# Folding a norm's factor into weights and evictions, and moving shared products into the expert pairs

## The chip, the cores and the metric

The kernel runs on one core of one Trainium2 chip. The metric is the device time of one launch in microseconds; less is better. The kernel before was timed three times: median 508.37 us, 507.75 to 508.88 us. One execution was recorded by the hardware profiler; every row shown below comes from it.

## The reference

One layer of a hybrid decoder on 512 tokens of width 1024, all in 32-bit floats. Cut to what matters here:

```python
h = h + rms_norm(mix, post_mix_norm)              # after attention and short convolution
t = rms_norm(h, pre_ffn_norm)                     # g_ffn: one factor per feature
g_idx  = top1(softmax(t @ w_group_router + b))    # one of 4 groups
e_idx  = top2 of the group's 8 experts            # weights normalised, times the group's
routed = sum over the 2 experts of  (silu(t @ w_gate[e]) * (t @ w_up[e]) * weight) @ w_down[e]
shared = (silu(t @ w_sh_gate) * (t @ w_sh_up)) @ w_sh_down
h = h + rms_norm(routed + shared, post_ffn_norm)
```

There are 32 experts of hidden width 256 and one shared expert of the same width. An expert's gate, up and down weights are 1 MB each.

## The kernel before

Tokens lie in four chunks of 128 (index c). The kernel computes projections and convolution (to about 95 us), attention (to about 185 us), the output projections (`pco`, `pao`), and then the part that the change touches:

- *Second norm.* For each chunk `chain_gen` adds the residual (`mix`), takes the sum of squares on ACT, raises it to -1/2 on GpSimd (`sst`), and multiplies the chunk by this factor per token and by `g_ffn` per feature in one DVE instruction (`x<-mix,sst,gb`). The result is stored in DRAM (`t_d`) for the gathers.
- *Router.* `router_gen` transposes the chunk on the tensor engine (`ptT`), copies it to `tT`, and multiplies by the router's weights (`plT`, then `plg`).
- *Routing.* `route` works on the DVE, first for chunks 0 and 1, then for 2 and 3: best group, two best experts, and, with small products (`pps`, `ptb`), the place of each token in its expert's list. It ends with the overflow tables (`code`), for experts with more than 64 tokens. Its scratch is the tile `rs`.
- *Shared expert.* `shared_gen` computes its gate and up products (`psh`: for each chunk 32 products, from the weight tiles (32, 0) and (32, 1) and from `tT`). They fill the tensor engine while routing goes on. Its down products (`psd`) come later in blocks, into the tiles `sho`.
- *Expert pairs.* `pairs_gen` treats two experts at a time, j and j + 16, each with up to 64 tokens, side by side in the tensor engine. Per pair: the gathered tokens `xg` are transposed (`pxt`) into `wk`; sixteen gate-up products follow in two halves, i = 0 and 1 (`pgu`); silu and weighting; the next pair's transposes; the hidden layer's transposes (`pht`, evicted by ACT into `wk`); eight down products (`pdn`, out to `yb`); and an indirect DMA sends the rows to `y_d`. The last pair stays on the chip (`ys`).
- *Tail.* `last_gen` adds up, chunk by chunk in PSUM (`pca`), the shared part (`inject`: a product with the identity), the last pair's rows (a product with a selection `sel`), and the two routed rows of each token, read back from `y_d` and added on the DVE (`kk`). Then the third norm: squares on ACT, the product with `g_post` (`tm`) and the variance (`var`) on the DVE, the power on GpSimd (`rf`), and a multiply-add with the residual `hb` on the DVE, stored to `out`.

*What sets the order.* All stages are generators. `run` asks each, in the order of its priority, when it could go on by a model of the engines (`Progress`), and lets the first go that can; so the order on each engine is fixed when the program is built. Buffers are 25 slots of 1 MB. `rel` gives slots back, and `pump` hands them in turn to the queue of weight loads: on SP, in a fixed order, each load behind the last use of the slot that it takes. A tile's name (e, i) is expert e's gate-up half 0 or 1, or its down weights (2); 32 is the shared expert.

Nearly all instructions bear one of two lines in the profile, L159 (the wrapper of the engines) and L314 (`pe`, the tensor engine), so they are told apart by the names of their tiles.

Of the kernel before, what the change touches and what calls it, by code (L numbers as in the profile page):

```python
# [45 lines left out]
S_AT = 2  # L46
S_GO = 2
# [118 lines left out]
def hymba_kernel(ctx: ExitStack, tc: tile.TileContext, xT, xmT, x, meta, cpk, pos, wqkv, wconv, wuq, wukv,  # L166
# [214 lines left out]
    Y.dma_start(mt[:NMETA, :D], meta)  # L381
    Y.dma_start(posi, pos)
# [528 lines left out]
    def finish(c):  # L911
# [25 lines left out]
        if c == NT - 1:  # L937
            rel(A["b"])
            Y.dma_start(wrt, wr)

# [4 lines left out]
    def out_split_gen():  # L945
# [10 lines left out]
        Y.dma_start(late["gb"][:, D:2 * D], g_ffn[None, :].to_broadcast([P, D]))  # L956
# [6 lines left out]
        keep(0)  # L963

# [38 lines left out]
    def attn_out_gen(c, mg):  # L1003
# [19 lines left out]
        if c == NT - 1:  # L1023
            rt["rs"], rt["xg"], sh["hs"] = take(["rs", "xg", "hs"], *(wo[k] for k in range(4)), *A["mg"])
# [4 lines left out]
    def chain_gen(c, ss):  # L1029
        gb, m = late["gb"], mix(c)  # L1030
# [12 lines left out]
        V.scalar_tensor_tensor(tt(c), m, sst[:, c, 2:3], gb[:, D:2 * D], op0=OP.mult, op1=OP.mult)  # L1043
        spawn(router_gen(c), 0 if c == NT - 1 else P_ROUTER)

    def router_gen(c):
# [14 lines left out]
        yield every(at(*(tT(k, c * P, (c + 1) * P) for k in (0, 4))), free_bank())  # L1061
# [22 lines left out]
    def shared_gen():  # L1084
        yield loaded((NE, 0), (NE, 1))
        w = [got((NE, i)) for i in range(2)]
        for c in range(NT):
# [13 lines left out]
        yield flag(rt, "idx")  # L1101
        sh["gu"] = True
# [8 lines left out]
        sh["out"] = reserve("sho0", "sho1")  # L1111
        yield lambda: 0.0 if len(sh["out"]) == 2 else INF
        yield at(hs_, wd)
        for c in range(NT):
            for half in range(2):
                yield free_bank(2)
                ps = bank("psd")
                for f in range(2):
                    mm(ps, hs[:, c, f, 1], wd[:, half * 1024 + f * 512:half * 1024 + (f + 1) * 512],
                       start=f == 0, stop=f == 1)  # L1120
                copy(acc(c)[:, half * 512:(half + 1) * 512], ps)
        rel(hs_, wd)
        sh["done"] = True
# [168 lines left out]
    def xpose(src, dst, by=S):  # L1292
        for q in range(2):
# [415 lines left out]
```

## Time and profile before

| | |
|---|---|
| timed runs, median | 508.37 us |
| profiled execution | 507.05 us |
| its span | 505.3 us |
| tensor engine busy | 479.0 us (95%) |
| DVE, ACT, GpSimd busy | 227.0, 163.4, 87.3 us |
| bytes moved by DMA | 151.30 MB |

The span goes from the first recorded instruction to the last; 1.75 us of the profiled execution lie outside it. In the page's list of slices each number stands for 12.6 us. In rows in order of time the first number is the start in us, the second the duration, and the bracket behind a row is the engine's idle time before it and what ended it. A group of like instructions that follow each other is one row with a count; a 32-bit product of the shared expert leaves two records.

### The profile page before, as it was taken

The numbers are of one execution on the slowest core, as the hardware profiler recorded it, in microseconds if no ns is written. First come the engines' busy times: TensorE is split into PE (matmuls) and PEld (weight loads), VectorE is DVE, ScalarE is ACT, GpSimd is POOL, SyncE is SP. The second block draws the span as 40 slices with busy tenths as digits, with TensorE's granted clock in tenths as the row PEclk, the third lists the DMA queues.
The fourth block names the chain that finished last, engine by engine and source line by source line (L and its number), as shares of the span: only waits on it lengthen the run. The fifth ranks groups of instructions, "written<-read, shape, count | busy, mean of one in ns | idle before, by whom it ended". The sixth has DMA issues, their size and how long they took to land. (4 is left out here: it accounts for less than half of the span.)

```text
span 505.3 us, 7279 instructions
## 1 busy us (share of the span) xinstructions
PE 479.0 (95%) x2780; PEld 303.0 (60%) x2780; DVE 227.0 (45%) x522; ACT 163.4 (32%) x334; POOL 87.3 (17%) x114
## 2 busy tenths in 40 slices
PE   8999999999999999997999999999999999988893
PEld 7998999788767788897963333433333333223251
DVE  6478789656877642678832111001111111111175
ACT  5775526445345642532122112211111111111131
POOL 2034234400000002460101111001111111100011
PEclk9999999999999999999999999999999999999997
DMA  8962240090207598399659999999999999999993
GB/s 291 401 248 83 84 167 0 35 382 2 84 2 279 220 354 325 134 382 381 242 239 421 417 423 420 422 416 421 420 420 419 420 420 417 420 419 424 405 365 150
DMA packets 30309, 151.30 MB, mean 299 GB/s; under 512 B 5480, under 2 KB 5864, under 8 KB 16192
## 3 DMA queue, kind: packets, MB, share of 16 engines
q1 hardware_dynamic: 24512, 138.43, 68.1%
q0 software_dynamic: 4464, 8.17, 4.4%
q10 hardware_dynamic: 1296, 4.21, 2.1%
q8 instruction: 23, 0.38, 0.3%
q14 instruction: 14, 0.11, 0.1%
HBM read 140.54 MB, written 18.35 MB: 314 GB/s over the span
## 5 line engine op out<-in xcount | busy, mean ns | idle before, releaser
L314 PE MATMUL pc<-xh,cw 128*128 128x256 f32 (+2 forms) x320 | 70.0, 309 | 0.0
L159 DVE SCALAR_TENSOR_TENSOR wk<-wk,wgt,pgu 128x256 f32<-128x256 f32 x16 | 7.7, 480 | 115.3 <-ACT wk L159 115.3
L314 PEld LDWEIGHTS pc<-xh,cw 128*128 128x128 f32 x320 | 52.3, 189 | 4.0 <-issue 1.3
L159 ACT ACTIVATE wk<-pgu 128x256 f32<-128x256 f32 x16 | 6.1, 383 | 133.7 <-PE pgu L314 133.7
L314 PE MATMUL pc<-xl,cw 128*128 128x256 f32 (+2 forms) x160 | 48.8, 305 | 0.0
L159 DVE COPY yb<-pdn 128x512 f32<-128x512 f32 x15 | 10.4, 692 | 60.4 <-PE pdn L314 60.4
L159 POOL DMA_INDIRECT xg<-t_d,idx x16 | 16.5, 1030 | 114.3 <-PE pxt L314 68.8
L159 POOL DMA_INDIRECT y_d<-yb,sidx x15 | 15.1, 1005 | 93.2 <-DVE yb L159 81.9
L314 PEld LDWEIGHTS pc<-xl,cw 128*128 128x128 f32 x160 | 30.4, 190 | 1.2
L159 ACT ACTIVATE att<-pS,nm 128x128 f32<-128x128 f32 (+3 forms) x32 | 16.9, 527 | 29.3 <-DVE nm L159 27.2
L314 PE MATMUL pS<-kT,qT 128*128 128x128 f32 (+3 forms) x64 | 22.7, 440 | 0.0
L159 POOL TENSOR_TENSOR sst<-rst,neghalf 128x1 f32<-128x1 f32 x12 | 7.5, 633 | 81.5 <-DVE rst L159 78.1
L314 PEld LDWEIGHTS pxt<-ident,xg 128*128 128x128 f32 x128 | 14.0, 140 | 11.3 <-issue 9.7
L314 PE MATMUL pco<-wo,cvh 128*128 128x512 f32 x64 | 20.6, 403 | 0.0
L314 PE MATMUL pao<-wo,mgh 128*128 128x512 f32 x64 | 20.0, 393 | 0.0
L159 POOL TENSOR_TENSOR cw<-ld conv,cw 128x1024 fp32r<-128x1024 f32 x6 | 15.7, 2618 | 18.5 <-ACT cw L159 18.5
L159 ACT ACTIVATE yb<-pdn 128x512 f32<-128x512 f32 x15 | 9.0, 597 | 29.2 <-PE pdn L314 29.2
L314 PE MATMUL psh<-tT,ld (32, 1)_1946 128*128 128x128 f32 x128 | 18.0, 279 | 0.0
L314 PE MATMUL psh<-tT,ld (32, 0)_1944 128*128 128x128 f32 x128 | 17.8, 279 | 0.0
L314 PE MATMUL pxt<-ident,xg 128*128 128x128 f32 x128 | 17.3, 278 | 0.0
L159 DVE TENSOR_REDUCE nm<-pS 128x1 f32<-128x128 f32 (+3 forms) x32 | 15.5, 484 | 1.7 <-PE pS L314 1.4
L314 PEld LDWEIGHTS psh<-tT,ld (32, 1)_1946 128*128 128x128 f32 x128 | 15.9, 192 | 0.2 <-issue 0.2
(486 smaller groups left out, 1190.5 us busy)
## 6 DMA issues: line engine op xcount, KB each, us to landing
ld conv<-in_wconv_dram SPq DMA_DIRECT2D x6, 1024.0 KB
ld out<-in_wout_dram SPq DMA_DIRECT2D x4, 1024.0 KB, 4.7
y_d<-sel SPq DMA_DIRECT2D x4, 1024.0 KB
ld kk<-y_d SPq DMA_DIRECT2D x4, 1024.0 KB
xs<-in_x_dram SPq DMA_DIRECT2D x4, 512.0 KB
x<-in_x_dram SPq DMA_DIRECT2D x4, 512.0 KB
h_d<-mix ACTq DMA_DIRECT2D x4, 512.0 KB
t_d<-x ACTq DMA_DIRECT2D x4, 512.0 KB, 10.2
```

What stands on the lines that cost most here:

```text
L159: r = f(*a, **k)
L314: f(o, *ins, **kw)
```

## The change

The factor `g_ffn` is no longer multiplied into the tokens. It is loaded as a tile with features on partitions (`gf`) and goes into the router's weights (one DVE product), into the shared expert's gate-up weights (eight ACT copies with a scale), and into the evictions of the gathered tokens' transposes (pair 0 and the overflow: eight ACT copies of 128 columns instead of two of 512; other pairs: two DVE products instead of one ACT and one DVE copy). The tokens' own factor becomes an ACT copy with a scale. `wk` is taken with the routing's tiles, and `yb` within pair 0. Pair 0 no longer waits for the flag `gu`. The shared down products are issued by the pairs: two a pair in pairs 3 to 6, one a pair in pairs 7 to 14, ahead of the pair's own down products. In the last pair the identity products of chunk 1 move into the two gate-up halves. In the tail the variance stands between the two products with `g_post`, and chunk 2 is stored ahead of chunk 3's statistics. Two numbers of the planner change: the pair at which the shared down weights are queued (`S_AT`), and from which they are used (`S_GO`).

```diff
-S_AT = 2
-S_GO = 2
+S_AT = 1
+S_GO = 3
...
+    gfr = mt[:8, 1536:1536 + P]
+    Y.dma_start(gfr, g_ffn.rearrange("(k p) -> k p", k=8))
...
+    gf = cp.tile([P, 8], F32, name="gf")
+    tr(pqm[:, 480:488], gfr, ident[:8, :8])
+    V.tensor_copy(gf, pqm[:, 480:488])
...
-        Y.dma_start(late["gb"][:, D:2 * D], g_ffn[None, :].to_broadcast([P, D]))
...
+        yield flag(cv, "wrt")
+        yield at(wrt)
+        w3 = wrt.rearrange("p (k n) -> p k n", k=8)
+        V.tensor_tensor(w3, w3, gf[:, :, None].to_broadcast([P, 8, 64]), op=OP.mult)
+        cv["wrg"] = True
...
-            rt["rs"], rt["xg"], sh["hs"] = take(["rs", "xg", "hs"], *(wo[k] for k in range(4)), *A["mg"])
+            rt["rs"], rt["xg"], rt["wk"], sh["hs"] = take(["rs", "xg", "wk", "hs"],
+                                                          *(wo[k] for k in range(4)), *A["mg"])
...
-        V.scalar_tensor_tensor(tt(c), m, sst[:, c, 2:3], gb[:, D:2 * D], op0=OP.mult, op1=OP.mult)
+        S.activation(tt(c), m, AF.Copy, scale=sst[:, c, 2:3])
...
+    def shared_scale_gen():
         yield loaded((NE, 0), (NE, 1))
         w = [got((NE, i)) for i in range(2)]
+        for k in range(8):
+            yield every(at(w[k // 4]), idle("ACT", early=1.0))
+            o = w[k // 4][:, (k % 4) * 512:(k % 4 + 1) * 512]
+            S.activation(o, o, AF.Copy, scale=gf[:, k:k + 1])
+        sh["w"] = w
...
         yield flag(cv, *(("lg", c) for c in range(NT)))
-        yield flag(rt, "idx")
-        sh["gu"] = True
         rel(*w, *tTs)
...
+    def shared_down():
+
+        hs, wd = sh["wd"]
+        c, half, f = sh["pieces"].pop(0)
...
+        mm(ps, hs[:, c, f, 1], wd[:, half * 1024 + f * 512:half * 1024 + (f + 1) * 512], start=f == 0, stop=f == 1)
...
     def xpose(src, dst, by=S):
...
-            if q and by is V:
-                V.tensor_copy(dst[:, q * 512:(q + 1) * 512], ps)
+            if by is V:
+                V.tensor_tensor(dst[:, q * 512:(q + 1) * 512].rearrange("p (k n) -> p k n", k=4),
+                                ps.rearrange("p (k n) -> p k n", k=4),
+                                gf[:, 4 * q:4 * q + 4, None].to_broadcast([P, 4, P]), op=OP.mult)
             else:
-                S.activation(dst[:, q * 512:(q + 1) * 512], ps, AF.Copy)
+                for k in range(4):
+                    S.activation(dst[:, q * 512 + k * P:q * 512 + (k + 1) * P], ps[:, k * P:(k + 1) * P], AF.Copy,
+                                 scale=gf[:, 4 * q + k:4 * q + k + 1])
...
     def pairs_gen():
-        box = reserve("wk", "yb")
-        ys = None
-        yield flag(sh, "gu")
-        yield lambda: 0.0 if box else INF
-        wk_, yb = box
-        rt["wk"] = wk_
+        wk_, yb, ys, box = rt["wk"], None, None, None
...
+                if j == NP - 1:
+                    yield every(flag(sh, "done"), free_bank(2))
+                    inject(1, (i,))
...
+                if j + i == 0:
+                    box = reserve("yb")
                 rel(*w)
...
+            if j >= S_GO:
+                yield every(flag(sh, "wd"), free_bank())
+                for n in range(2 if j < S_GO + 4 else 1):
+                    if sh["pieces"]:
+                        if "evict" in sh:
+                            shared_out()
+                        shared_down()
...
-        yield free_bank(2)
-        inject(1)
...
+            if c == NT - 1:
+                store(c - 1)
             for half in range(2):
                 S.activation(rt["jk"], pa[c, half], AF.Square, accum_out=ss[:, 2 * c + half:2 * c + half + 1])
-                V.tensor_tensor(tmc(c, HALF[half]), pa[c, half], gp[:, HALF[half]], op=OP.mult)
+            V.tensor_tensor(tmc(c, HALF[0]), pa[c, 0], gp[:, HALF[0]], op=OP.mult)
...
+            V.tensor_tensor(tmc(c, HALF[1]), pa[c, 1], gp[:, HALF[1]], op=OP.mult)
```

*The tensor engine around the transposes of chunks 2 and 3* (`x_1941` before, `x_1944` now; `upb` and `onesb` are the small position products). Before:

```order
L314 MATMUL ptT<-ident,x_1941 128x128 x8
L314 MATMUL psh<-tT_2021,ld (32, 0)_1944 128x128
L314 MATMUL ptT<-ident,x_1941 128x128 x8
...
L314 MATMUL pps<-rs,upb 128x32
L314 MATMUL psh<-tT_2021,ld (32, 0)_1944 128x128 x2
L314 MATMUL psh<-tT_2022,ld (32, 1)_1946 128x128 x2
L314 MATMUL plT<-tT_2021,m_77 64x128 x4
```

Now:

```order
L314 MATMUL pps<-rs,upb 128x32
L314 MATMUL psh<-tT_2030,ld (32, 0)_1947 128x128 x2
L314 MATMUL psh<-tT_2031,ld (32, 1)_1949 128x128 x4
L314 MATMUL psh<-tT_2030,ld (32, 0)_1947 128x128 x2
L314 MATMUL ptT<-ident,x_1944 128x128 x16
...
L314 MATMUL psh<-tT_2030,ld (32, 0)_1947 128x128 x2
L314 MATMUL psh<-tT_2031,ld (32, 1)_1949 128x128 x2
L314 MATMUL plT<-tT_2030,m_77 64x128 x4
```

The position products moved from behind the transposes to in front of them, with eight shared products between.

*The loads on SP from the last one before the shared expert's weights come free.* Before:

```order
L159 DMA ld (18, 2)_2418<-in_we_dram 128x2048
L159 DMA ld (32, 2)_2605<-in_we_dram 128x2048
L159 DMA ld (19, 0)_2652<-in_we_dram 128x2048
L159 DMA ld (3, 0)_2654<-in_we_dram 128x2048
L159 DMA ld (19, 1)_2680<-in_we_dram 128x2048
```

Now:

```order
L159 DMA ld (2, 2)_2628<-in_we_dram 128x2048
L159 DMA ld (18, 2)_2681<-in_we_dram 128x2048
L159 DMA ld (19, 0)_2691<-in_we_dram 128x2048
L159 DMA ld (3, 0)_2693<-in_we_dram 128x2048
L159 DMA ld (19, 1)_2734<-in_we_dram 128x2048
L159 DMA ld (3, 1)_2736<-in_we_dram 128x2048
```

(32, 2) went forward by six places, so as many loads as before stand ahead of (18, 2). By the waits of the built program, the four loads behind (18, 2) waited before for the shared products, their tokens and the routing's scratch; now (18, 2), (19, 0) and (3, 0) wait for products of pair 0's gate-up, (19, 1) and (3, 1) for its down products, and the buffers of the shared weights and their tokens go to (4, 1), (20, 1), (4, 2) and (20, 2).

*The DVE at the end of the tail* (`tm_3715` and `tm_3734` are the tile of chunks 2 and 3; `ld hb` the residual). Before:

```order
L159 TENSOR_TENSOR tm_3715<-pca,ld gp 128x512 x2
L159 TENSOR_SCALAR var<-ssf 128x1
L159 SCALAR_TENSOR_TENSOR var<-ssf,var 128x1
L159 SCALAR_TENSOR_TENSOR ld hb_3662<-tm_3715,rf,ld hb_3662 128x512 x4
```

Now:

```order
L159 SCALAR_TENSOR_TENSOR ld hb_3681<-tm_3734,rf,ld hb_3681 128x512 x2
L159 TENSOR_TENSOR tm_3734<-pca,ld gp 128x512
L159 TENSOR_SCALAR var<-ssf 128x1
L159 SCALAR_TENSOR_TENSOR var<-ssf,var 128x1
L159 TENSOR_TENSOR tm_3734<-pca,ld gp 128x512
L159 SCALAR_TENSOR_TENSOR ld hb_3681<-tm_3734,rf,ld hb_3681 128x512 x2
```

Two of the last four multiply-adds moved ahead of chunk 3's statistics, and one product with `g_post` behind the variance.

## Rows read from the trace of the kernel before

**Rows 1.** The page: busy us, share, instructions; GB/s in 40 slices.

```profile
PE 479.0 (95%) x2780; PEld 303.0 (60%) x2780; DVE 227.0 (45%) x522; ACT 163.4 (32%) x334; POOL 87.3 (17%) x114
...
GB/s 291 401 248 83 84 167 0 35 382 2 84 2 279 220 354 325 134 382 381 242 239 421 417 423 420 422 416 421 420 420 419 420 420 417 420 419 424 405 365 150
```

**Rows 2.** Sums by stretch: busy us (instructions) per engine, clock, DMA share, GB/s.

```profile
250.00:260.00 10.00, 9.69 (x82) 8.66 (x82) 7.37 (x31) 3.00 (x5) 0.99 (x1) 1.00 0.24 90
260.00:270.00 10.00, 8.82 (x46) 3.42 (x44) 2.46 (x4) 2.75 (x6) 0.99 (x1) 1.00 1.01 418
...
400.00:450.00 50.00, 47.01 (x222) 17.02 (x220) 7.45 (x12) 7.84 (x16) 6.08 (x7) 1.00 1.02 420
```

**Rows 3.** Waits of the tensor engine, 258 to 481 us: total, times, longest.

```profile
PE pdn L314 <- ACT wk L159: 8.1, 14, 1.2
PE pgu L314 <- DMA ld (30, 1)_3435<-in_we_dram: 1.3, 1, 1.3
...
PE pgu L314 <- DMA ld (30, 0)_3419<-in_we_dram: 0.3, 1, 0.3
```

**Rows 4.** Order of time, SP: issues of weight loads (start, duration, tile).

```profile
237.12 0.44 SPq L159 DMA_DIRECT2D ld (18, 2)_2418<-in_we_dram  x1
256.68 0.33 SPq L159 DMA_DIRECT2D ld (32, 2)_2605<-in_we_dram  x1
...
258.33 0.53 SPq L159 DMA_DIRECT2D ld (19, 1)_2680<-in_we_dram  x1
262.40 0.33 SPq L159 DMA_DIRECT2D ld (3, 1)_2682<-in_we_dram  x1
...
265.83 0.33 SPq L159 DMA_DIRECT2D ld (3, 2)_2694<-in_we_dram  x1
272.13 0.33 SPq L159 DMA_DIRECT2D ld (4, 0)_2733<-in_we_dram  x1
```

**Rows 5.** Order of time, GpSimd: the gather of pair 2.

```profile
258.69 0.99 POOL L159 DMA_INDIRECT xg<-t_d,idx  x1 [10.80 <-PE pxt L314]
```

**Rows 6.** Order of time, DVE: routing.

```profile
225.27 1.43 DVE L159 SCALAR_TENSOR_TENSOR x<-mix,sst,gb 128x1024 f32<-128x1024 f32 x1
...
229.71 1.28 DVE L159 SCALAR_TENSOR_TENSOR x<-mix,sst,gb 128x1024 f32<-128x1024 f32 x1
...
236.38 0.17 DVE L159 TENSOR_REDUCE rs<-plg 128x2 f32<-128x8 f32 x1
...
257.65 0.17 DVE L159 TENSOR_TENSOR code<-code,rs 128x8 f32<-128x8 f32 x1
```

**Rows 7.** Order of time, tensor engine: transposes, position, shared and router products.

```profile
231.13 1.06 PE L314 MATMUL ptT<-ident,x 128*128 128x128 f32 x8 [2.75 <-DVE rs L159]
232.03 0.20 PE L314 MATMUL pps<-rs,upb 128*128 128x32 bf16 x2
...
232.19 0.69 PE L314 MATMUL psh<-tT,ld (32, 0)_1944 128*128 128x128 f32 x4
...
233.25 1.97 PE L314 MATMUL plT<-tT,m 128*64 128x128 f32 x32
```

**Rows 8.** Order of time, pair 0: ACT's evictions, first gate-up and down products.

```profile
258.07 1.09 ACT L159 ACTIVATE wk<-pxt 128x512 f32<-128x512 f32 x2
...
258.73 0.64 PE L314 MATMUL pgu<-ld (0, 0)_1948,wk 128*64 128x512 f32 x1 [0.31 <-ACT wk L159]
...
268.45 0.64 PE L314 MATMUL pdn<-ld (0, 2)_1972,wk 128*64 128x512 f32 x1 [1.18 <-ACT wk L159]
```

**Rows 9.** Order of time, the tail: tensor engine, DVE, GpSimd.

```profile
482.18 1.49 PE L314 MATMUL pca<-ys,sel 128*128 128x512 f32 x4
...
481.50 0.69 DVE L159 TENSOR_TENSOR ys<-pdn,ys 128x512 fp32r<-128x512 f32 x1 [1.02 <-ACT ys L159]
...
498.43 2.74 DVE L159 SCALAR_TENSOR_TENSOR ld hb<-tm,rf,ld hb 128x512 f32<-128x512 f32 x4
...
498.59 1.00 POOL L159 TENSOR_TENSOR rf<-var,neghalf 128x1 f32<-128x1 f32 x1 [3.10 <-DVE var L159]
```

More of the change, by code (lines that the diff above doesn't have):

```diff
@@ L939, in finish @@
             Y.dma_start(wrt, wr)
+            cv["wrt"] = True
     wo = {}
@@ L1023, in attn_out_gen @@
         if c == NT - 1:
-            rt["rs"], rt["xg"], sh["hs"] = take(["rs", "xg", "hs"], *(wo[k] for k in range(4)), *A["mg"])
+            rt["rs"], rt["xg"], rt["wk"], sh["hs"] = take(["rs", "xg", "wk", "hs"],
+                                                          *(wo[k] for k in range(4)), *A["mg"])
+            G.memset(sh["hs"][:, 0:1], 0.0)
             rt["place"] = rt["rs"][:, 1792:1920]
@@ L1029, in chain_gen @@
     def chain_gen(c, ss):
-        gb, m = late["gb"], mix(c)
+        m = mix(c)
         yield at(ss)
@@ L1060, in router_gen @@
             held.append(rt["lg"])
-        yield every(at(*(tT(k, c * P, (c + 1) * P) for k in (0, 4))), free_bank())
+        yield every(flag(cv, "wrg"), at(*(tT(k, c * P, (c + 1) * P) for k in (0, 4))), free_bank())
         ps = bank("plT")
@@ L1082, in acc, with shared_gen @@
         return sh["out"][c // 2][:, (c % 2) * D:(c % 2 + 1) * D]
-    def shared_gen():
+    def shared_scale_gen():
         yield loaded((NE, 0), (NE, 1))
         w = [got((NE, i)) for i in range(2)]
+        for k in range(8):
[3 more added lines that the diff above has]
+        sh["w"] = w
+    def shared_gen():
+        yield flag(sh, "w")
+        w = sh["w"]
         for c in range(NT):
@@ L1110, in shared_gen, with shared_out @@
         wd = got((NE, 2))
-        sh["out"] = reserve("sho0", "sho1")
-        yield lambda: 0.0 if len(sh["out"]) == 2 else INF
+        sh["out"] = reserve("sho0")
+        yield lambda: 0.0 if sh["out"] else INF
         yield at(hs_, wd)
-        for c in range(NT):
-            for half in range(2):
-                yield free_bank(2)
[L1117 to L1123, printed above, removed]
+        sh["pieces"] = [(c, half, f) for c in range(NT) for half in range(2) for f in range(2)]
+        sh["wd"] = hs, wd
+    def shared_down():
+        hs, wd = sh["wd"]
+        c, half, f = sh["pieces"].pop(0)
+        if f == 0:
+            sh["ps"] = bank("psd")
+            held.append(sh["ps"])
+        ps = sh["ps"]
+        mm(ps, hs[:, c, f, 1], wd[:, half * 1024 + f * 512:half * 1024 + (f + 1) * 512], start=f == 0, stop=f == 1)
+        if f == 1:
+            held.remove(ps)
+            sh["evict"] = (c, half, ps)
+        if (c, half, f) == (1, 1, 0):
+            sh["out2"] = reserve("sho1")
+    def shared_out():
+        if "evict" not in sh:
+            return
+        c, half, ps = sh.pop("evict")
+        if c == 2 and half == 0:
+            sh["out"] += sh["out2"]
+        copy(acc(c)[:, half * 512:(half + 1) * 512], ps)
+        if not sh["pieces"]:
+            rel(sh["hs"], sh["wd"][1])
+            sh["done"] = True
     rowp = cp.tile([P, 2, NT], F32, name="rowp")
@@ L1483, in pairs_gen @@
                          [w[q][:, k * 512:(k + 1) * 512] for q in range(2)], i + k == 0, i + k == 4)
+                if j + i == 0:
+                    box = reserve("yb")
                 rel(*w)
+            if j == 0:
+                yield lambda: 0.0 if box else INF
+                yb = box[0]
             hidden(ps, wgt[:, j:j + 1], sg, hd)
             sh["silu"] = True
-            if j == S_GO:
+            if j == S_GO - 1:
                 sh["go"] = True
@@ L1523, in pairs_gen @@
             rel(*w)
+            if j >= S_GO:
+                if "out2" in sh and len(sh["out"]) == 1:
+                    yield lambda: 0.0 if sh["out2"] else INF
+                shared_out()
             if j < first:
@@ L1540, in hymba_kernel, with inject @@
     pa = {}
-    def inject(c):
-        for half in range(2):
+    def inject(c, halves=(0, 1)):
+        for half in halves:
             pa[c, half] = bank("pca")
@@ L1561, in last_gen @@
         rel(*w)
-        yield free_bank(2)
-        inject(1)
         tm = reserve("tm0", "tm1")
@@ L1608, in last_gen @@
             G.tensor_tensor(rf[:, c:c + 1], v[:, 1:2], neghalf[:, 0:1], op=OP.pow)
+            V.tensor_tensor(tmc(c, HALF[1]), pa[c, 1], gp[:, HALF[1]], op=OP.mult)
             for half in range(2):
                 held.remove(pa[c, half])
-            if c:
-                yield loaded(f"hb{(c - 1) // 2}") if c % 2 else None
+            if c % 2 == 0:
+                yield loaded(f"hb{c // 2}")
+            if 0 < c < NT - 1:
                 store(c - 1)
@@ L1624, in hymba_kernel @@
     spawn(route(), P_ROUTE)
+    spawn(shared_scale_gen(), 1)
     spawn(shared_gen(), 8)
```

## The prediction, made before the result was known

> **What bounds the kernel now.** I read the page's busy shares first, then the sums by stretch, the waits, and last the issues of loads in order of time. The page alone points at the tensor engine: it is busy for 95% of the span [rows 1]. The sums by stretch say otherwise. The DMA share stands at 1.01 from 260 us and still at 1.02 up to 450 us, with 418 and 420 GB/s; the one hole is the stretch from 250 to 260 us, with a share of 0.24 and 90 GB/s [rows 2]. So the weights come in one unbroken stream from about 258 us on. The tensor engine's waits show where the two meet: in the first pairs it waits only for ACT's eviction of the transposed hidden layer (8.1 us in 14 waits), and in pairs 13 to 15 it waits five times for weights that have just landed, the last before the second half of pair 15 [rows 3] (the longest and the shortest of the five stand there). The weights set the end: whatever delays that stream delays the last pair and the tail by as much, and whatever saves tensor time inside the pairs saves nothing.
>
> When the stream starts is set by buffers. The last load before the hole is issued at 237.12 us; the next four are issued from 256.68 to 258.33 us, when the shared expert's gate-up products have read their weights and transposed tokens for the last time; then two loads follow each pair's gate-up and down halves: 262.40 us, 265.83 us, 272.13 us [rows 4]. Pair 0's first product stands at 258.73 us [rows 8], so these three come 3.7, 7.1 and 13.4 us after it.
>
> **The change part by part.** The sum is made against the profiled execution: 507.05 us, of which 505.3 us are span and 1.75 us lie around it. The median of the timed runs, 508.37 us, is 1.32 us above that; I carry the difference over unchanged.
>
> 1. *The feature factor leaves the DVE.* Two of the four multiplications that go stood in the routing of the first two chunks, 1.43 and 1.28 us [rows 6]; ACT now does the same step as a scaled copy, near 1.1 us, since its two evictions of 512 columns take 1.09 us [rows 8], and ACT stands idle there. This could bring the second half of the routing (236.38 us in the row) forward by 2.7 us, and by up to 0.9 us more because a third multiplication before the routing goes too. But the tensor engine's order moves with it. Before, the transposes of chunks 2 and 3 stand ahead of the small position products, and from the shared products behind these to the router products pass 1.06 us (232.19 to 233.25 us [rows 7]). Now the position products stand first, and behind them eight shared products, all sixteen transposes and four more shared products come ahead of the router products. A row counts each shared product twice, so one takes about 0.26 us (1.06 over four); twelve make 3.2 us, and sixteen transposes at 0.11 us (231.13 to 232.03 us for eight [rows 7]) make 1.8 us: 5.0 instead of 1.06, or 3.9 us more. Against 2.7 to 3.6 us gained that leaves +0.3 to +1.2 us if every microsecond counts, and -1.5 us if a good part of these products runs while the engine would have waited anyway. I take 0: the second half of the routing and the tables behind it end where they did, the last step that pair 0 needs at 257.8 us (257.65 plus 0.17 [rows 6]).
>
> 2. *The start of pair 0.* Pair 0's transposes now stand sixteen shared products earlier, but the buffer of their result is the one of the routing scratch, so ACT's first eviction waits for the overflow tables on the DVE. The eviction is cut into eight pieces of 128 columns; the first product needs only the first. One piece costs at least nothing and at most the 0.55 us of one whole eviction (two took 1.09 us [rows 8]); I take the middle, 0.3 us. So the first product comes at about 258.3 us instead of 258.73, bounds 256.8 to 259.5. The eleven shared products that stay over are put into the waits of pairs 0 and 1 (1.2 us before the first down product [rows 8]) and cost at most 0.5 us there, off the path, because the weights are.
>
> 3. *The stream restarts later.* This is the main term. The shared gate-up weights and transposed tokens are now read until pair 1, so their four buffers come free some 22 us after pair 0's start (13.4 us for pair 0, 7.1 for pair 1's gate-up, then its transposes) instead of before it, and the loads that stood first in the hole have nothing to go into. The next buffers are those of pair 0's own first half, 3.7 us after its first product: 262.0 us instead of 256.68, **+5.3 us**. One gather of tokens (0.5 MB, issued at 258.69 us [rows 5], in the full stream) now falls in the hole: 0.52 MB at 420 GB/s, **-1.25 us**. Then the stream starves once more: three tiles and a gather last 3 x 2.5 + 1.25 = 8.75 us (1.05 MB at 420 GB/s is 2.5 us), from about 263.3 us on (1.3 us after the issue, as 256.68 us against a share that fills at about 258) to 272.1 us; the next loads wait for pair 0's down products, 13.4 us after its start or 271.7 us, and flow from 273.0 us: **+0.9 us**. From there buffers come free faster than the stream fills them (a pair takes the tensor engine about 13 us and its six tiles, gather and send 17.5 us of stream). Sum: +4.95 us; with the bounds of step 2, 3.4 to 6.2 us.
>
> 4. *Shared down products in the pairs, other transposes' evictions, loads that go.* All off the path while weights set the pace: 0. If that cover were gone, the down products' place would be worth most of the 8.1 us of rows 3; that is a rival below. The multiplication of the router's weights and the eight scaled copies of the shared weights fall between 185 and 216 us, where DVE and ACT wait for tensor products: 0, at worst one eviction's 0.55 us if one lands in front of an eviction that the engine waits for. The broadcast load that goes lies far before the hole: 0.
>
> 5. *The last pair and the tail.* The chunk-1 product with the identity leaves the place behind the last down product and goes into pair 15's waits for weights. It gives little: it stood beside the DVE's last eviction (481.50 plus 0.69 us), and the products behind it start when that is done, at 482.18 us [rows 9]. I take -0.1, bounds -0.7 to 0. At the very end, the DVE row that ends last holds four multiply-adds of 2.74 us in all, two of them chunk 2's, from 498.43 us [rows 9]. Chunk 2's two now go before chunk 3's statistics. The power on GpSimd (1.00 us from 498.59 us) is then the path, but it starts one 0.69 us multiplication earlier, which now runs beside it. So the last two multiply-adds start after 497.9 + 1.0 instead of 499.8 us: **-0.9 us**, bounds -1.4 to 0. Together -1.0.
>
> The sum is +4.95 - 1.0 = about +3.9 us: 510.95 us in a profile, **512.2 us** as a median.
>
> Can the stream catch up? From 258 us on no slice of the page shows more than 424 GB/s, and most show 419 to 421 [rows 1]: it runs at its top already, and I give it nothing back.
>
> One rule speaks the other way. The rows show the tensor engine waiting 8.1 us in the pairs for ACT, beside a full stream [rows 2, 3]. The Trainium skill, Perfetto Trace Analysis, section Optimization Strategies, says that the goal is in general to keep the matmul engine as busy as possible; by that rule the filled waits would be the gain. That is the first rival.
>
> **The rivals.**
> *The tensor engine is the bound, and its filled waits pay* (faster). Place: the wait before each pair's down products. Price: twelve of the fourteen waits, 6.9 us, and the tail's 1.0: 500.5 us. It would decide if the weights lay ready when the engine asks. For it: 95% busy, and no wait for weights in pairs 0 to 12. Against it: the five waits of rows 3. It could only hold in part, say half, 504 us.
> *The routing gets all of the DVE's gain* (no change). If the reordered products hide in idle tensor time, pair 0 starts 3 us earlier, at 255.3 us; the stream then shifts by +4.95 - 3.0 = +2.0 us and the time by +1.0 or less, about 509.0 us. For it: the tensor engine waited 2.75 us before those transposes [rows 7]. Against it: the products behind the position products are many.
> *The routing gets later* (slower still). If the 5.0 us count in full, pair 0 starts 1.2 us later: 513.4 us.
>
> **How the numbers follow.** Chances: the starved stream as worked out 0.60, the later routing 0.14, the early routing 0.11, filled waits that pay 0.15. About 0.2%, 1.0 us, is what a measurement of this kernel can tell from no change. The first two cases give slower, 0.74; the third same, 0.11; the fourth faster, 0.15. The range goes from 507.8 us, the early routing with both of the tail's bounds (2.0 - 2.1 us on 508.37) less half a microsecond for the median's own spread, to 514.5 us, the late routing with no gain in the tail; the faster case stays outside.
>
> **What would show it.** In the changed kernel's profile: the first load after the hole at 262 us or so, taken up after a product of pair 0, and only three tiles issued before pair 0's down products; the DMA share low from 250 to 262 us and a second dip near 272 us; more waits for weights in the last pairs, fewer for ACT. The DVE's second routing half near 236.4 us would show step 1; under 234 us, the early rival. The last pair's second half would start near 475 us and the end follow it one microsecond sooner than now. If the stream is full at 258 us, or pair 15 waits for no weights, the forecast is wrong.

## The result: 3.2% slower, more than four times the loss that was forecast

The changed kernel takes 525.19 us in the median of four runs (524.49 to 525.81), beside 508.62 us (507.75 to 509.11) for the kernel before on the same chip: a ratio of 1.0318, 95% interval 1.0292 to 1.0344. The direction was forecast, the size was not: +16.6 us instead of +3.9, and 525.19 lies above the range's end of 514.5. The profiled execution took 525.7 us with a span of 524.0 us, 18.7 us more than the span before.

The list of slices already says that there are two places, not one. Slices count 13.1 us each here (the span over 40); a digit gives the busy share, or the granted clock, in tenths (9 is 90% or more).

```profile
PE   8968999999999999999969999999999888898993
...
PEclk9978999999999999999979999999999999999998
...
GB/s 289 401 215 56 36 71 161 1 214 189 81 2 110 316 278 295 185 339 393 280 25 323 409 423 422 422 421 419 421 420 421 423 419 418 421 421 423 390 394 163
```

The tensor engine loses busy time and clock in the third and fourth slice (26 to 52 us), where nothing was expected, and again in the 21st (262 to 275 us), where the stream of weights now has its hole: 25 GB/s.

**The first 50 us.** On ACT and then on DVE, in order of time (start, duration, and in the bracket the idle time before it and what ended it):

```profile
26.61 1.06 ACT L159 ACTIVATE m<-xs 128x1024 bf16<-128x1024 f32 x1 [10.85 <-DVE ssx L159]
```

```profile
17.10 0.29 DVE L159 TENSOR_TENSOR kvs<-mt,kvs 128x128 fp32r<-128x128 f32 x1
26.39 0.17 DVE L159 COPY gf<-pqm 128x8 f32<-128x8 f32 x1 [8.99 <-PE pqm L314]
26.51 0.07 DVE L159 MEMSET ssx<- 128x16 f32 x1
29.92 1.23 DVE L159 TENSOR_TENSOR cw<-ld conv,cw 128x1024 fp32r<-128x1024 f32 x1 [3.34 <-ACT cw L159]
```

In the kernel before, the same two rows stand 9.3 us earlier:

```profile
17.22 0.07 DVE L159 MEMSET ssx<- 128x16 f32 x1
...
17.32 1.06 ACT L159 ACTIVATE m<-xs 128x1024 bf16<-128x1024 f32 x1 [1.69 <-DVE ssx L159]
```

The 0.17 us copy of the feature factor waits 8.99 us for its transposition, which stands on the tensor engine behind all the first projection's products (`pq`, `pqm`). Behind the copy, on the same engine, stands the memset of `ssx`, which needs nothing; ACT's squares write into `ssx` and wait for it; the splits of the convolution's weights (`cw`) stand on ACT behind those squares; and the convolution's products wait for the splits. The tensor engine's waits (total, times, longest) from 15 to 60 us, of which the kernel before has none:

```profile
PE pc L314 <- ACT cw L159: 3.6, 1, 3.6
PE pc L314 <- DVE ctmp L159: 2.4, 1, 2.4
PE pc L314 <- DVE cw L159: 0.5, 1, 0.5
```

These 6.5 us become more, and the granted clock is lower in the same stretches. The sums by stretch, columns as in [rows 2]:

```profile
20.00:30.00 10.00, 6.41 (x50) 6.05 (x48) 0.27 (x3) 3.36 (x6) 0.00 (x0) 0.91 1.03 420
30.00:40.00 10.00, 9.28 (x56) 8.61 (x56) 5.27 (x8) 9.68 (x28) 1.20 (x1) 0.75 0.28 118
40.00:50.00 10.00, 7.81 (x50) 7.62 (x51) 7.04 (x24) 3.56 (x6) 4.21 (x2) 0.83 0.01 3
```

Before, these three stretches show 10.00 us busy each at a clock of 1.00. The clock has two levels, 0.50 and 1.00 (1.2 and 2.4 GHz); a value between them is a stretch with some of both. Three stretches at 0.91, 0.75 and 0.83 lose at most 5.1 us by the clock, part of it within the gaps: an estimate that leaves room for the 4.0 us by which the delay exceeds the waits. From the attention on everything stands 10.5 us later at unchanged distances: its first product at 119.39 us instead of 108.93, the last output projection at 226.09 instead of 215.57.

**The hole in the stream.** Pair 0's eviction and products, answering to [rows 8], and the loads, answering to [rows 4]:

```profile
268.81 2.18 ACT L159 ACTIVATE wk<-pxt,gf 128x128 f32<-128x128 f32 x8 [9.66 <-DVE code L159]
```

```profile
269.23 1.12 PE L314 MATMUL pgu<-ld (0, 0)_1951,wk 128*64 128x512 f32 x1 [4.41 <-ACT wk L159]
...
270.14 1.06 PE L314 MATMUL pgu<-ld (0, 0)_1951,wk 128*64 128x512 f32 x1
...
274.59 0.59 PE L314 MATMUL pgu<-ld (0, 0)_1951,wk 128*64 128x512 f32 x1
```

```profile
250.35 0.42 SPq L159 DMA_DIRECT2D ld (2, 2)_2628<-in_we_dram  x1
275.22 0.33 SPq L159 DMA_DIRECT2D ld (18, 2)_2681<-in_we_dram  x1
...
278.65 0.33 SPq L159 DMA_DIRECT2D ld (3, 0)_2693<-in_we_dram  x1
284.81 0.33 SPq L159 DMA_DIRECT2D ld (19, 1)_2734<-in_we_dram  x1
```

Pair 0's first product comes 10.50 us later than before, at 269.23 us; the loads restart 6.0 us behind it, at 275.22 us, where before they restarted 2.05 us ahead of it. The forecast had 3.7 us. The other 2.3 us are the clock: after a wait of 4.41 us the first products run at half of it, the lower level (0.85 us from one to the next instead of 0.43), as the stretches show:

```profile
264.00:266.00 2.00, 0.82 (x8) 0.63 (x6) 1.93 (x3) 0.00 (x0) 1.44 (x1) 1.00 0.00 0
...
268.00:270.00 2.00, 0.77 (x2) 0.30 (x4) 0.77 (x6) 1.19 (x5) 0.00 (x0) 0.50 0.00 0
270.00:272.00 2.00, 2.00 (x8) 0.61 (x6) 0.00 (x0) 1.98 (x5) 0.00 (x0) 0.50 0.00 0
...
274.00:276.00 2.00, 2.00 (x12) 0.68 (x10) 0.00 (x0) 0.00 (x0) 0.00 (x0) 1.00 0.00 0
```

**The end.** Pair 15's second half starts 18.9 us later (489.74 us against 470.86). The last two multiply-adds on DVE start at 517.51 us and take 1.41 us; in [rows 9] the last two of the four ended at 501.17. So they end 17.75 us later, 1.1 us less than that.

The sum by the two traces, start to end: early 10.5; restart against pair 0's first product 8.0 (2.05 + 5.99), of which 2.3 clock; a gather in the hole -1.25; second dip of the stream 1.6 (what is left of the 18.9, with the gather at its forecast price); tail -1.1, and +0.9 because the span ends 5.1 us behind the last multiply-add instead of 4.1. That makes 18.7 us, the difference of the spans; since the dip is a remainder, the agreement is no proof of it. The dip itself can be seen: the four stretches of 2 us from 284 to 292 us show 242, 295, 377 and 375 GB/s, by 420 GB/s 1.9 us of missing stream.

### The profile page after: what moved, and what is told of

Its sections match the earlier page's. It is cut to its first block, busy times and chain, and to the rows that moved or that the text cites. A ratio compares the mean times of both kernels' runs of the same rounds, so it can differ in the third digit from the quotient of the medians.

```text
span 524.0 us, 7300 instructions
## 1 busy us (share of the span) xinstructions
PE 491.4 (94%) x2781; PEld 306.5 (59%) x2781; DVE 230.8 (44%) x536; ACT 164.8 (31%) x337; POOL 82.0 (16%) x114
## 4 chain that ended last, share of the span: by engine, by line
PE 69%; DMA 20%; DVE 7%; ACT 1%; issue 1%; SPq 0%; DVEq 0%; ACTq 0%; POOLq 0%
PE pgu L314 14%; PE pc L314 13%; PE pdn L314 7%; PE pco L314 4%; PE pao L314 4%; DMA ld (30, 1)_3454<-in_we_dram 4%; DMA ld (26, 1)_3186<-in_we_dram 4%; DMA ld (13, 0)_3375<-in_we_dram 4%; DMA ld (11, 2)_3291<-in_we_dram 4%; PE pS L314 4%; PE pO L314 3%; DVE rs L159 3%; PE pq L314 3%; PE psh L314 3%; DMA ld kk<-y_d 2%; PE pqh L314 2%
## 5 line engine op out<-in xcount | busy, mean ns | idle before, releaser
L314 PE MATMUL pc<-xh,cw 128*128 128x256 f32 (+2 forms) x320 | 73.4, 319 | 6.5 <-ACT cw L159 3.6
L314 PEld LDWEIGHTS pc<-xh,cw 128*128 128x128 f32 x320 | 54.8, 198 | 11.2 <-ACT cw L159 3.7
L314 PE MATMUL pc<-xl,cw 128*128 128x256 f32 (+2 forms) x160 | 50.1, 313 | 0.0
L314 PEld LDWEIGHTS pc<-xl,cw 128*128 128x128 f32 x160 | 32.0, 200 | 1.2
L159 DVE TENSOR_TENSOR wk<-pxt,gf 128x512 f32<-128x512 f32 x30 | 19.2, 683 | 0.0
L314 PE MATMUL psh<-tT,ld (32, 0)_1947 128*128 128x128 f32 x128 | 18.4, 280 | 0.0
L314 PE MATMUL psh<-tT,ld (32, 1)_1949 128*128 128x128 f32 x128 | 18.4, 278 | 0.0
L314 PEld LDWEIGHTS psh<-tT,ld (32, 1)_1949 128*128 128x128 f32 x128 | 16.1, 192 | 0.2 <-issue 0.2
```

The costliest lines, as they stand in the source:

```text
L159: r = f(*a, **k)
L314: f(o, *ins, **kw)
```

## The experiments

Theory A has two parts: the copy of `gf` ahead of the memset makes the early loss, and the late restart of the stream makes the rest. Each of the nine runs takes away or adds one piece. The ratios are to the kernel before, timed beside each run: medians 508.88 us in experiments 1, 2, 4 and 5, 508.9 in 3 and 6 to 8, 509.31 in 9.

**1. The copy placed later** (the changed kernel, otherwise untouched).

```diff
-    gf = cp.tile([P, 8], F32, name="gf")
-    tr(pqm[:, 480:488], gfr, ident[:8, :8])
-    V.tensor_copy(gf, pqm[:, 480:488])
...
     conv_split(1)
+    gf = cp.tile([P, 8], F32, name="gf")
+    tr(pqm[:, 480:488], gfr, ident[:8, :8])
+    V.tensor_copy(gf, pqm[:, 480:488])
```

> The changed kernel with one edit: the transposition and the DVE copy of the feature factor (gf) stand behind the second group of convolution-weight splits instead of ahead of the DVE's memset of ssx. Theory A (the copy gf<-pqm, first in line on DVE, holds back the memset that ACT's squares wait for, and through them the splits of the convolution's weights and the tensor engine's clock): the first convolution product returns from 29.94 to about 26 us, pS to where it stood before the change (10.5 us earlier), and the time falls by 10.5 us from 525.2 to 514.7 us (513.5 to 516). Rival B (the 10.5 us come from the extra load among the first ones, or from the order that the planner chose around it): the first convolution product stays near 30 us and the time within 2 us of 525. In both, the hole in the weight stream and the halved clock ahead of pair 0 stay: the loads restart 6 us after pair 0's first product.

516.7 us (516.36 to 518.33), ratio to the kernel before 1.0171 (1.0140 to 1.0203). 8.5 us of the 16.6 are gone; theory A had 10.5. Rival B falls: ACT's squares start on time again,

```profile
17.16 1.06 ACT L159 ACTIVATE m<-xs 128x1024 bf16<-128x1024 f32 x1 [1.68 <-DVE ssx L159]
```

and the first convolution product stands at 26.07 us (26.05 before). The missing 2 us: the last output projection is still 1.7 us late, see experiment 9.

**2. The copy alone, in the kernel before.** Its diff is the added load, transposition and copy of the change; nothing uses `gf`.

> The kernel before, with only the 8x128 load of the feature factor, its transposition and its DVE copy added where the changed kernel has them; the result (gf) isn't used. Theory A: these three small instructions alone cost 10.5 us in the first 60 us: 508.6 + 10.5 = 519.1 us (517.5 to 520.5), with ACT waiting some 10 us for ssx at 16 to 27 us, and from 60 us on every step stands 10.5 us later at unchanged distances. Rival B (the early loss needs something else of the change): 508.6 us within 1 us, or a part of it.

517.67 us (516.09 to 518.9), ratio 1.0169 (1.0137 to 1.0202): three small instructions cost 8.8 us. ACT shows the same wait as the changed kernel:

```profile
27.72 1.06 ACT L159 ACTIVATE m<-xs 128x1024 bf16<-128x1024 f32 x1 [11.09 <-DVE ssx L159]
```

From the first attention product (120.70 us, +11.77) to pair 15's second half (482.68, +11.82) the distance to the kernel before stays the same, so the stream gives nothing back. That its +11.8 us exceed the medians' 8.8 is due to the executions that were profiled: here the longest of the four (518.9 us), in the kernel before one 1.8 us below its median.

**3. The memset ahead of the copy.**

```diff
+    ssx = cp.tile([P, 16], F32, name="ssx")
+    V.memset(ssx, 1.0)
     gf = cp.tile([P, 8], F32, name="gf")
     tr(pqm[:, 480:488], gfr, ident[:8, :8])
     V.tensor_copy(gf, pqm[:, 480:488])
...
-    ssx = cp.tile([P, 16], F32, name="ssx")
-    V.memset(ssx, 1.0)
```

> The changed kernel with one edit: the tile ssx is made and set to one ahead of the copy of the feature factor instead of behind it; the copy itself stays where it is, ahead of DVE's splits of the convolution's weights. Theory A (the chain is copy, memset, ACT's squares, ACT's splits, products): ACT's squares start at about 17.3 us again instead of 26.6, ACT's first split at about 20 us, and only DVE's first split (21.2 us in the kernel before) still stands behind the copy at 26.4 us, so the first convolution products are held up by 1 to 2 us instead of 10.5 in the end: 525.2 - 8.5 to 9.5 = 515.7 to 516.7 us (515 to 518), as late_gf (516.7). Rival B (DVE's own splits behind the copy are the link, the memset is not): ACT's squares start early but the loss stays near 9 us, 522 to 525 us.

519.64 us (519.08 to 520.31), ratio 1.0209 (1.0180 to 1.0237). Neither number was met. The memset is the larger link: moving it alone gives back 5.6 of the 8.5 us. Of the 2.9 us to experiment 1, the traces put 2.0 in the first part (the first attention product at 111.86 us instead of 109.85): DVE's own splits still queue behind the copy, and the tensor engine waits 1.0 us for one. Another 1.1 us come at pair 0, where the loads restart 6.47 us behind its first product instead of 5.38, after a like wait and at a clock of 0.50 from 262 to 268 us.

```profile
17.52 0.07 DVE L159 MEMSET ssx<- 128x16 f32 x1
26.73 0.17 DVE L159 COPY gf<-pqm 128x8 f32<-128x8 f32 x1 [9.14 <-PE pqm L314]
26.82 1.22 DVE L159 TENSOR_TENSOR cw<-ld conv,cw 128x1024 fp32r<-128x1024 f32 x1
```

That split stood at 21.22 us before. Here the clock stays at 1.00 from 20 to 50 us, while in experiment 2 it falls to 0.67 in one stretch.

**4. The old release of the buffers**, on top of experiment 1.

```diff
         yield flag(cv, *(("lg", c) for c in range(NT)))
+        yield flag(rt, "idx")
+        sh["gu"] = True
         rel(*w, *tTs)
...
         wk_, yb, ys, box = rt["wk"], None, None, None
+        yield flag(sh, "gu")
```

> The kernel of late_gf, and besides the shared expert's gate-up products are finished and their four buffers given back before pair 0 starts, as in the kernel before (the flag is waited for again); so the loads (19,0) and (19,1) wait for the shared products and the tokens' copies again. Theory A (what is left of the loss after late_gf is the late restart of the stream of weights and the second dip behind it): the loads restart about 2 us before pair 0's first product instead of 6 us behind it, the DMA share is above 0.9 from 260 us on, and the time falls by 6 to 8 us from 514.7 to about 507.5 us (506 to 509.5). Rival B (the filled waits were never going to pay, and the rest of the loss is tensor time: the scaled evictions, the clock): the stream restarts early but the time falls by under 2 us, to 513 or more.

507.69 us (507.12 to 509.05), ratio 0.9987 (0.9973 to 1.0002): 9.0 us below experiment 1 and level with the kernel before, so theory A. The loads restart ahead of pair 0's first product (261.07 us) again, and the stream is full from 260 us:

```profile
257.36 0.33 SPq L159 DMA_DIRECT2D ld (18, 2)_2662<-in_we_dram  x1
```

```profile
250.00:260.00 10.00, 9.03 (x92) 8.62 (x90) 8.79 (x40) 1.20 (x2) 1.20 (x2) 1.00 0.38 107
260.00:270.00 10.00, 8.55 (x42) 3.27 (x42) 1.99 (x8) 5.22 (x13) 0.90 (x2) 1.00 1.02 425
270.00:280.00 10.00, 9.90 (x46) 3.38 (x48) 2.23 (x4) 0.64 (x2) 1.45 (x2) 1.00 1.01 415
```

In experiment 1 the same three stretches moved less:

```profile
250.00:260.00 10.00, 5.98 (x64) 5.79 (x63) 8.75 (x40) 0.35 (x2) 1.45 (x1) 1.00 0.29 84
260.00:270.00 10.00, 9.62 (x40) 3.50 (x41) 0.39 (x2) 3.81 (x10) 0.00 (x0) 0.83 0.33 117
270.00:280.00 10.00, 10.00 (x56) 4.44 (x56) 2.03 (x4) 0.98 (x2) 2.00 (x2) 1.00 0.91 351
```

That is (107 + 425 + 415) - (84 + 117 + 351) = 395 GB/s over 10 us, or 3.95 MB; at 420 GB/s 9.4 us, beside 9.0 measured at the end. The stream's loss and the kernel's agree, as they must if the stream sets the end; experiment 6 tests it in another way. The 9.0 us hold the clock's part too: in experiment 4 the tensor engine waits 2.0 us ahead of pair 0 instead of 4.4, and the clock stays at 1.00.

**5. The tensor engine kept busy through its wait**, on top of experiment 1: 36 transposes of the identity ahead of pair 0's first product.

```diff
                 if ps is None:
                     ps = bank("pgu")
+                if j + i == 0:
+                    for _ in range(36):
+                        T.transpose(ps[:, 0:P], ident, ident)
```

> The kernel of late_gf with 36 idle transposes of the identity, some 4 us of tensor work, between the shared products and pair 0's first gate-up product, into a bank that this product overwrites: the engine works while it would wait for the scaled evictions. Theory A (the granted clock falls to half in that wait and stays there for pair 0's first 4 to 5 us, 0.86 us a step instead of 0.43, and the buffers that its products free come 2.3 us later): the clock stays at 1.00, the distance from pair 0's first gate-up product to pair 0's last falls from 9.3 to about 7 us, and the time is 2.3 us below late_gf, 512.4 us (511.5 to 513.5). Rival B (the lost clock is made up by the stream, or the products are slow for another cause): the same time as late_gf, 514.7 us within 1 us. If the dummies outlast the wait, pair 0's first product comes up to 1 us later and the gain is that much smaller.

515.78 us (515.08 to 516.04), ratio 1.0141 (1.0113 to 1.0169); 0.9 us below experiment 1, not 2.3. The clock stays at 1.00, and the first product (261.37 us) is followed by the restart 3.67 us later, the forecast's distance to the hundredth:

```profile
261.37 0.64 PE L314 MATMUL pgu<-ld (0, 0)_1951,wk 128*64 128x512 f32 x1 [0.48 <-ACT wk L159]
261.85 0.59 PE L314 MATMUL pgu<-ld (0, 0)_1951,wk 128*64 128x512 f32 x1
```

```profile
265.04 0.33 SPq L159 DMA_DIRECT2D ld (18, 2)_2717<-in_we_dram  x1
```

In experiment 1 the restart came 5.38 us behind the first product (260.38 and 265.76 us), so the clock is worth 1.7 us there rather than 2.3. The first product itself comes 1.0 us later (261.37 us), so the restart gains only 0.7 us, near the 0.9 of the medians; the intervals overlap, so the time alone would not show a gain.

**6. Pair 0's transposed tokens in a buffer of their own**, on top of experiment 1, so the evictions no longer wait for the overflow tables.

```diff
-            rt["rs"], rt["xg"], rt["wk"], sh["hs"] = take(["rs", "xg", "wk", "hs"],
-                                                          *(wo[k] for k in range(4)), *A["mg"])
+            Slots.avail += [PR.last(t) for t in (*(wo[k] for k in range(4)), *A["mg"])]
+            rt["rs"] = slot("rs")
...
+            rt["xg"], rt["wk"], sh["hs"] = slot("xg"), slot("wk"), slot("hs")
```

> The kernel of late_gf, and the buffer of pair 0's transposed tokens (wk) is no longer the one of the routing's scratch, so ACT's eight scaled evictions need not wait for the overflow tables. Theory A (the stream restarts when pair 0's first half frees buffers, so whatever brings pair 0 forward brings the whole stream forward): pair 0's first product about 4 us earlier (256 to 257 us instead of 260.4), no fall of the clock, the restart 5 to 7 us earlier than in late_gf (259 to 261 us instead of 265.8), and the time 5 to 7 us lower, 510.5 us (509 to 512). Rival B (the late restart is not what sets the end, or another step holds pair 0 where it is): 515 us or more.

511.79 us (511.25 to 512.26), ratio 1.0057 (1.0038 to 1.0076). Pair 0's first product stands at 255.84 us, 4.5 us earlier than in experiment 1, the wait and the fall of the clock are gone, and the loads restart at 259.87 instead of 265.76 us. The time follows by 4.9 us. That is less than the 5.9 us of the restart for two reasons that the trace shows: with the slots handed out in another way, the load (2, 2), which stood before the hole in experiment 1 (241.40 us), stands behind it (1.05 MB, 2.5 us at 420 GB/s); and the second dip is gone (no stretch of 2 us from 262 to 294 us below 377 GB/s). 5.9 - 2.5 + 1.6 makes 5.0. Another way of moving the stream's start, the same effect at the end.

**7. The tail alone, in the kernel before** (step 5 of the prediction; its diff is the `inject`, `last_gen` part of the change).

> The kernel before with only step 5 of the change: the identity product of chunk 1 in pair 15's halves, chunk 2 stored ahead of chunk 3's statistics, the variance between the two products with g_post. The prediction's step 5 gives -1.0 us: 507.9 us against 508.9. By the profile of the changed kernel, where the last multiply-adds end 1.1 us earlier against the last pair's products but the span ends 5.1 us instead of 4.1 us behind them, only -0.2 us: 508.7 us.

508.0 us (506.45 to 509.08), ratio 0.9978 (0.9965 to 0.9992): -0.9 us of medians, and 0.4 to 1.8 us less by the interval. The forecast of -1.0 holds; the -0.2 does not: here the span ends 4.1 us behind the last multiply-add (500.93 plus 1.41, to 506.4 us), as in the kernel before, so the +0.9 at the changed kernel's end belongs to another part of the change.

**8. The tail and the spread shared products, in the kernel before.** Beside experiment 7's edit, the diff of `shared_down`, `shared_out` and their calls in `pairs_gen`.

> The kernel of tail_only, and besides the shared down products are issued by the pairs (two a pair in pairs 3 to 6, one a pair in 7 to 14) as in the changed kernel; the rest is the kernel before. Theory A (weights set the end): the waits of the tensor engine for ACT ahead of the down products fall from 8.1 us to about 2, the waits for weights in the last pairs grow by as much, and the time is that of tail_only within 0.5 us. Rival B (filled waits pay): the time falls by 3 to 6 us against tail_only.

508.42 us (506.72 to 511.07), ratio 0.9995 (0.9977 to 1.0012): no gain over experiment 7. The waits [rows 3] show why. The tensor engine waits 2.8 us for ACT instead of 8.1, and the engine reaches pair 5 at 326.88 us instead of the kernel before's 332.48, yet pair 15's second half starts at 473.60 us, no earlier than experiment 7's 473.02:

```profile
PE pdn L314 <- ACT wk L159: 2.8, 4, 1.2
PE pgu L314 <- DMA ld (13, 1)_3368<-in_we_dram: 1.4, 1, 1.4
PE pgu L314 <- DMA ld (28, 1)_3301<-in_we_dram: 1.4, 1, 1.4
PE pgu L314 <- DMA ld (30, 1)_3435<-in_we_dram: 1.3, 1, 1.3
```

The waits for weights begin in pair 12 now, with (28, 1), instead of pair 13: the engine gets ahead of the stream sooner and waits there. The listed waits do not grow by as much as was expected: with (13, 0) they come to 4.5 us, 1.8 more than in experiment 7, where 5.3 us less are waited for ACT. Part of the rest is hidden in busy time, since one expert of a pair can start alone: in pair 12 (12, 1) starts at 423.12 us and (28, 1) at 425.52, and only 1.4 us of that count as a wait. How much it is in all was not added up.

**9. The copy out of the first 60 us altogether**, on top of experiment 4.

```diff
-    gfr = mt[:8, 1536:1536 + P]
-    Y.dma_start(gfr, g_ffn.rearrange("(k p) -> k p", k=8))
...
-    tr(pqm[:, 480:488], gfr, ident[:8, :8])
-    V.tensor_copy(gf, pqm[:, 480:488])
...
         Y.dma_start(late["gb"][:, :D], g_mix[None, :].to_broadcast([P, D]))
+        Y.dma_start(late["gb"][:8, D:D + P], g_ffn.rearrange("(k p) -> k p", k=8))
...
+        yield every(at(late["gb"]), free_bank())
+        ps = bank("pgf")
+        tr(ps[:, 0:8], late["gb"][:8, D:D + P], ident[:8, :8])
+        V.tensor_copy(gf, ps[:, 0:8])
...
```

> The kernel of late_gf_old_slots, with the feature factor loaded and transposed only behind the output projections' weights (about 185 us), into a half of a tile that the change left empty and through a bank of its own; so the first 60 us hold the same instructions in the same order as in the kernel before. Theory A (the rest of the early loss, 1.0 to 1.7 us at the first pk in late_gf and late_gf_old_slots, comes from the order of the splits around the product ctmp): that rest goes, and the time is 507.7 - 1.2 = 506.5 us (505.5 to 507.5), below the kernel before. Rival B (that rest is the scatter between executions): 507.7 us within 0.7.

506.21 us (505.97 to 507.5), ratio 0.9945 (0.9922 to 0.9968): 0.3 to 0.8% faster than the kernel before, and faster than experiment 4, whose interval of 0.9973 to 1.0002 it misses by 0.0005, on another chip. That favours theory A, if narrowly: even where the copy costs no wait of its own, its place changed the order that the planner chose on DVE. In experiments 1 and 4 two splits stand ahead of the products `ctmp`, and the tensor engine waits for `ctmp`, which it did not before; here is experiment 4's wait, of which 0.3 us are left in experiment 9:

```profile
PE pc L314 <- DVE ctmp L159: 1.3, 1, 1.3
```

Where the 0.5% come from is open. The tail of experiment 7 is not among them as it stood there: from pair 15's second half to the end of the span pass 34.2 us here, 33.4 in experiment 7 and 34.4 in the kernel before. And the two traces are only 0.8 us apart (506.23 and 507.05 us), while the medians are 3.1 us apart, so most of the gain lies in executions that no trace shows.

## Why the prediction was right in direction and wrong in size

*The step that failed is the fourth.* It priced what the change adds or takes away outside the hole at 0 and named the router's weights, the scaled copies and the broadcast load that goes. The three instructions that make `gf`, which stand in the diff ahead of all of them, have no term in it. Measured by medians they cost 8.5 us (experiment 1) and 8.8 us (experiment 2), more than half of the whole. The price was not in their durations (0.17 us) but in what stands behind them on their engine. The direction is not luck: without the copy's loss the kernel is still 1.7% slower (experiment 1), by the mechanism of step 3. For the copy the order of the program would have sufficed: a copy that waits for the tensor engine, in front of a memset that waits for nothing. The Trainium skill, PSUM — Partial Sum Buffer, section Engine vs sequencer instructions, says that the queues of ScalarE, VectorE and GpSimdE are strictly first in, first out; the trace agrees, with the memset 9.29 us behind its place before.

*Step 1, the routing ends where it did.* Right in sum. From the last output projection to the overflow tables pass 41.96 us (226.09 to 268.05) against 41.60 before: +0.4, where bounds of -1.5 to +1.2 had been set. The two opposite shifts are there, smaller than forecast as far as the traces tell them apart: the routing's first half starts 1.3 us sooner (7.36 us behind the last output projection instead of 8.63), its second half 1.6 us later behind the first (13.80 instead of 12.18). The sign of the +0.4 says little, since the kernel before's own routing took 43.0 and 43.1 us in the traces of experiments 7 and 8.

*Step 2, pair 0 by -0.4 us.* Right against the tables: first product 1.18 us behind `code` instead of 1.56.

*Step 3, the restart.* The mechanism is right, and it is the other half of the loss: experiments 4 and 6 move the stream's start and the end follows. But +4.95 us were forecast, and giving the buffers back as before is worth 9.0 (experiment 4). Three tiles before pair 0's down products and a second dip came as told. The distance of 3.7 us between first product and restart was met at full clock (3.67 in experiment 5, 4.03 in experiment 6). Two sizes were off. The clock had no term: the wait of 4.4 us for ACT's evictions, which step 2 itself creates by putting them behind the tables, brings the granted clock to 0.50, and the buffers that pair 0 frees come 1.7 us (experiment 1) to 2.3 us later (the changed kernel). The second dip took 1.6 to 1.9 us instead of 0.9.

*Step 4, filled waits give nothing.* Right in this: experiment 8 shows no gain from them, and the first rival falls with it. The rule of the Trainium skill that was quoted for this rival (Perfetto Trace Analysis, section Optimization Strategies) does not decide here: the engine's waits for ACT fell from 8.1 to 2.8 us and the time stayed.

*Step 5.* Right for the tail itself: -1.0 forecast, -0.9 measured (experiment 7). Its inner sizes were partly luck: counted from ACT's last square the power on GpSimd starts 0.4 us sooner (1.36 us behind it instead of 1.75), not 0.7, but it takes 0.55 us instead of the 1.00 that the sum had. The 0.9 us that the changed kernel loses behind the last multiply-add had no term.

*The rivals.* The early routing did not come: the routing takes 0.4 us more, not 3 less. (Its +1.0 us on 508.37 would make 509.4, not 509.0 us.) The later routing of +1.2 us did not come either. None of them looked at the first 60 us, so the range had no room for 8.5 us.

## What to carry to other kernels

Price an added instruction by what queues behind it on its engine, not by its duration: a 0.17 us copy that waits 9 us for its input in front of a memset cost 1.7% here; placing it behind the second group of splits gave 8.5 us back, and in experiment 9, where it left that stage altogether, the time fell by another 1.5. Where a stream of loads sets the end, give buffers back before spending them on filler work: the shared products that were to fill the tensor engine's waits held the buffers that the stream needed, and cost 9 us, the clock's part included. And look over the whole diff for instructions in other stages before summing the stage that it seems to be about.

## What the runs showed that was not expected

- A wait of 4.41 us with no tensor work ahead of pair 0 brought the granted clock from 1.00 to 0.50, and it came back only some 4.5 us after the products had started; in another place a shorter gap did the same in some traces (last point); 36 idle transposes (4.09 us) in the same place kept it at 1.00. In the first 50 us, where gaps of 3.6 and 2.4 us stood, stretches of 10 us show 0.91, 0.75 and 0.83, and 6.5 us of waits became a delay of 10.5 us.
- The span ends 4.9 to 5.2 us behind the last multiply-add in every kernel that folds the factor into weights and evictions (the changed one, experiments 1, 3 to 6 and 9), and 4.1 to 4.2 us in the three that do not (experiments 2, 7, 8) and in the kernel before. So about 0.9 us at the very end come with another part of the change than the tail's order and the spread products. In the traces of the kernel before and of the changed one 0.8 of it stands in the stores to `out`: each 256 KB store lands 2.1 us after its issue before, 2.9 us now. Why, no run here shows.
- Single traces of the same program scatter, and here the clock is the cause: the second half of the routing begins 12.18 us after the first in the kernel before and 13.61 us in experiment 7, whose instructions up to there are the same. In both the tensor engine waits 2.75 us ahead of the transposes of chunks 2 and 3 [rows 7]; in experiment 7 the granted clock falls with that wait. Of the four kernels with this order, experiment 8 shows the fall too (13.72 us), experiment 2 does not (12.19 us). With the change's order the longest wait there is 0.5 us, and none of the seven traces with it shows this fall. Differences under 2 us between two traces therefore say little unless the medians or several traces agree. The stretch in the kernel before, then in experiment 7:

```profile
232.00:234.00 2.00, 2.00 (x30) 1.87 (x30) 1.91 (x8) 1.83 (x6) 0.00 (x0) 1.00 1.01 414
```

```profile
232.00:234.00 2.00, 2.00 (x15) 1.94 (x15) 1.07 (x6) 1.29 (x4) 0.00 (x0) 0.50 1.03 420
```
